# Storing gates and spatial results in turned blocks, and a new order of the attention

## The chip, the cores and the metric

The kernel runs on one core of a Trainium2 chip. The metric is the device time of one execution in microseconds. [...]

## The reference

One layer of a decoder trunk with 512 tokens of 2048 channels, in float32. A vector `c` conditions the layer. Two token mixers stand side by side, a latent attention and a chunked spatial gating unit, and a learned gate each merges them:

```python
mod = silu(c) @ w_ada + b_ada;  shift, scale, gate = split(mod, 3)
h = rmsnorm(x, attn_norm_g) * (1 + scale) + shift
q_lat, kv_lat, k_rope, z_mla, u, v, z_sgu, g_mla, g_sgu = split(h @ w_in)
q = rmsnorm(q_lat) @ w_uq           # 16 heads, 128 plain + 64 rotary columns
kv = rmsnorm(kv_lat) @ w_ukv        # 16 heads, 128 key + 128 value columns
y_mla = causal_attention(q, k, v_mla) * silu(z_mla)
y_sgu = u * (tril(w_spatial) @ rmsnorm(v) + b_spatial) * silu(z_sgu)   # chunks of 128 tokens
merged = sigmoid(g_mla) * y_mla + sigmoid(g_sgu) * y_sgu
out = rmsnorm(x + gate * (merged @ w_out), final_norm_g)
```

## The kernel before

Every float32 product is made of three products of a reduced type: each operand is split into a high part (a cast on ScalarE) and a low part (the rest, a subtraction on VectorE). A 128-column slice of weights against 512 tokens is one matmul of 512 columns.

The kernel has three long stages. The first projects the latents and some plain columns. The **block stage** makes the wide projections v, u, the three gate inputs and the two z with fewer products than the plain way: seven products of half size in place of eight, so that a block of two groups of 512 channels runs through 28 steps (the list `V7`) of twelve matmuls each. Eleven blocks (`BLOCKS`) follow one another. Around each step, a dictionary of events, filled by a planner that spreads the work with `place` and `on`, tells what ScalarE, VectorE and the queues do in that step; events of the phase `LOAD` are transfers on SP's queue. Weights are loaded some five steps before their first use. Results of a group of four heads are kept in two tiles `held[...]` of [128 tokens, 2, 512 channels], one for each half of the tokens. For c in 0 to 3, `t_store` writes the finished spatial results to `t_d[c]` in DRAM, and for c in 0 to 2, `g_out` writes the finished gate of the attention branch (silu of z times sigmoid of g) to `gt_d[c]`; each is one transfer of 512 KB for each half. The last gate, c = 2, is finished only when the attention begins, by the list `last_gates`.

The **attention** takes the 16 heads in order. Its matmuls in head h are: the scores of head h; in an odd head the values of two heads (`vproj`); the query projection of head h + 1 (`qproj`); in an even head the rotary projection of the next pair (`rproj`); the key projection of head h + 1 (`kproj`); and the product of head h - 1's shares with its values (`pv`). Each engine works through its queue in the order in which the program writes it. The softmax adds a mask, finds the maximum, takes exponentials (ScalarE, with their sums), turns the shares in blocks of 32 x 32 on VectorE and stores them to `p_d`; `turned_load` brings them back so that the blocks stand in turned places, `turned_split` makes high and low parts of them on ScalarE and GpSimd, and `pv` uses them one head later. The spatial results come back in the same way: `fetch_blocks` loads each head's [channels, tokens] tile in four transfers of 32 x 16 runs of 128 bytes, and VectorE turns each 32 x 32 block (L1779). The gate comes back with tokens on the partitions, in runs of 512 bytes. There the reciprocal sums of the softmax are multiplied into it (four scalings on ScalarE, L1818), and four transposes on TensorE (`turn`, L1721) bring it to [channels, tokens], with a copy out of PSUM (L1778). Heads 12 to 15 (`GATED = 12`) have a gate that is already turned; there VectorE scales the shares.

The weights of a projection come through `Stream`: three raw buffers, a high and a low part in two places, loaded by SP in order, split in order. `get(i, ahead)` asks for granule i and splits `ahead` more. `merge_a` multiplies the attention by the gate and adds the spatial result; the `finish` that it queues splits the sum later for the output projection. `pieces_at` sums the pieces of the conditioning's gate between the heads on VectorE (L148).

The third stage is the output projection (`out_granule`) with the residual and the last norm.

Of the kernel before, what the change touches and what calls it, by code (L numbers as in the profile page):

```python
# [20 lines left out]
P = 128  # L21
# [116 lines left out]
def trunk_layer(ctx, tc, xT, xn, c, vecs, pos, wada, w1, w2, wv, wv3, wv4, wh, wh15, wq, wqr, wk, wvv, wo, wsT, bsp, gfin, out,  # L138
# [106 lines left out]
    gt_d = [scratch(f"gt_d{i}", [NB, P, S]) for i in range(3)]  # L245
    t_d = [scratch(f"t_d{i}", [NB, P, S]) for i in range(4)]
# [684 lines left out]
    def g_out(c, half):  # L931
        DMA.dma_start(gt_d[c][2 * half:2 * half + 2].rearrange("n p w -> p n w"), held["z", c, half])

    last_gates = []
    for b in range(1, len(BLOCKS)):
# [21 lines left out]
        if ta == "z":  # L957
            for half in range(2):
                s_ = max(ready[ta, ca, half], ready[tb_, cb, half]) + 1
                if b == len(BLOCKS) - 1:  # L960
                    last_gates.append(lambda c=ca, half=half: (g_gate(c, half, DVE if half else nc.gpsimd), g_out(c, half)))
# [62 lines left out]
    def t_store(c, half):  # L1024
        DMA.dma_start(t_d[c][2 * half:2 * half + 2].rearrange("n p w -> p n w"), held["u", c, half])
# [12 lines left out]
    for g in range(H):  # L1038
# [433 lines left out]
    for n, tag in (("krh", "hh10"), ("krl", "hl10"), ("m1", "hh11"), ("m2", "hl11"), ("r", "hh12"), ("qsa", "hl12"),  # L1472
                   ("qsb", "hh13"), ("pt1", "hl13"), ("th0", "hh14"), ("tl0", "hl14"), ("th1", "hh15"), ("tl1", "hl15")):
        place[n] = (hp.p, tag)
    for n, tag in zip(("vh0", "vl0", "qh", "ql", "kh", "kl", "vh1", "vl1", "pt3", "pt2", "th2"), range(11)):
        place[n] = (latp.p, f"lat{tag}")
# [13 lines left out]
    for key, at_ in ready.items():  # L1490
        if at_ >= 0:
            squash(key)
# [6 lines left out]
    gd = Scope("gdots")  # L1499
    cq.clear()  # L1500
    piece_at = lambda i: piece_load(i, lambda: nt(gd.p, [P, S], F32, "piece", bufs=2))

    def pieces_at(h):
        k = n_early + sum(PIECES[:h])
        for i in range(k, k + PIECES[h]):
# [3 lines left out]
            if i > n_early and pieces[i][0] != pieces[i - 1][0]:  # L1509
                quarter_after(i)  # L1510

# [16 lines left out]
    def fetch(h):  # L1528

        gt[h] = nt((ga if h < 8 else g2p).p, [P, S], F32, f"g{h}")  # L1530
        if h < GATED:
            DMA.dma_start(gt[h].rearrange("p (n w) -> p n w", n=NB),
                          gt_d[h // 4][:, :, h % 4 * P:(h % 4 + 1) * P].rearrange("n p w -> p n w"))
# [4 lines left out]

    def fetch_blocks(h):

        vt[h] = nt(bp.p, [P, S], F32, f"b{h}")
        rows = t_d[h // 4].rearrange("n (a i) w -> i (n a) w", i=SQ)
        for b in range(P // SQ):
            o = h % 4 * P + b * SQ
            DMA.dma_start(vt[h][b * SQ:(b + 1) * SQ].rearrange("i (m j) -> i m j", j=SQ), rows[:, :, o:o + SQ])
# [16 lines left out]
    def qproj(h, meanwhile=None, then=None):  # L1562
        wH, wL = get(gq[h])
# [462 lines left out]
```

## Time and profile before

| what | us |
|---|---|
| median of 3 runs | 1538.77 (1537.94 to 1539.0) |
| profiled execution, time | 1538.12 |
| profiled execution, span | 1536.2 |
| TensorE busy | 1521.3 |
| VectorE busy | 1233.6 |
| ScalarE busy | 804.9 |
| GpSimd busy | 169.2 |

The span goes from the first to the last instruction; the profiled execution's time is 1.9 us longer. Times in the rows count from the start of the span. The block stage ends at 1072 us, the attention at about 1341 us. Ends of matmuls are modelled, so that one matmul's time overlaps the next; the pitch is read from start to start.

### The profile page before, as it was taken

What the parts mean: (1) busy time and instruction counts of PE and PEld (TensorE: products, weight loads), DVE (VectorE), ACT (ScalarE), POOL (GpSimd) and SP (SyncE); (2) the same over time, 40 slices, a digit from 0 to 9 for tenths busy, and PEclk for the clock granted to TensorE, in tenths of its full rate; (3) what the DMA queues carried; (4) which work ended last, traced back from release to release, by engine and by line L of the source; (5) the groups of instructions that cost most, each with busy time, mean ns of one, the idle gap of its engine ahead of it and who ended that gap; (6) DMA issues with size and microseconds to landing.
All of it is one profiled execution on the core that took longest, in us unless ns stands there. A gap on an engine that the chain in (4) does not pass through costs nothing.

```text
span 1536.2 us, 20578 instructions
## 1 busy us (share of the span) xinstructions
PE 1521.3 (99%) x7152; PEld 1272.9 (83%) x7152; DVE 1233.6 (80%) x1676; ACT 804.9 (52%) x1276; POOL 169.2 (11%) x161
## 2 busy tenths in 40 slices
PE   9999999999999999999999999999999999999997
PEld 7888878888888888888888888888888888888886
DVE  8989797768787889887888787878789889965753
ACT  4444555546555546455555565557666666532331
POOL 0000000101010000011010101010122223221120
PEclk9999999999999999999999999999999999999999
DMA  9979776858886786878686867777788888759832
GB/s 374 385 271 352 235 215 173 237 147 238 248 223 187 211 231 199 228 214 217 198 207 187 225 207 188 239 191 215 201 204 191 202 190 190 193 148 339 281 105 110
DMA packets 368922, 337.93 MB, mean 220 GB/s; under 512 B 133689, under 2 KB 313969, under 8 KB 363697
## 3 DMA queue, kind: packets, MB, share of 16 engines
q1 hardware_dynamic: 345906, 313.54, 66.0%
q0 software_dynamic: 22912, 23.07, 9.8%
q8 instruction: 56, 0.92, 0.3%
q14 instruction: 48, 0.39, 0.1%
HBM read 302.38 MB, written 34.17 MB: 219 GB/s over the span
## 4 chain that ended last, share of the span: by engine, by line
PE 92%; DVE 3%; DMA 2%; SPq 1%; ACT 1%; issue 1%; DVEq 0%; ACTq 0%
PE ps L1457 18%; PE ps L1458 18%; PE ps L1455 18%; PE ps L463 5%; PE ps L158 3%; PE ps L1769 3%; PE ps L1771 3%; PE ps L1772 3%; PE ps L159 3%; PE ps L157 3%; PE ps L1557 3%; PE ps L1558 2%; PE ps L1560 2%; PE ps L472 2%; PE ps L473 2%; PE ps L475 1%
## 5 line engine op out<-in xcount | busy, mean ns | idle before, releaser
L145 DVE TENSOR_TENSOR X<-X,X 128x1024 fp32r<-128x1024 f32 (+2 forms) x111 | 130.5, 1183 | 28.5 <-ACT X L694 27.1
L694 ACT CAST w0h<-X 128x1024 fp32r<-128x1024 f32 x70 | 73.6, 1052 | 95.4 <-PE ps L1458 51.8
L694 ACT CAST X<-X 128x1024 fp32r<-128x1024 f32 x70 | 73.6, 1052 | 93.7 <-PE ps L1458 56.4
L694 ACT CAST w1h<-X 128x1024 fp32r<-128x1024 f32 x69 | 72.5, 1051 | 76.0 <-PE ps L1458 39.6
L145 DVE TENSOR_TENSOR w0l<-X,w0h 128x1024 fp32r<-128x1024 f32 x70 | 85.6, 1222 | 28.5 <-ACT w0h L694 28.3
L145 DVE TENSOR_TENSOR w1l<-X,w1h 128x1024 fp32r<-128x1024 f32 x69 | 84.3, 1221 | 24.4 <-ACT w1h L694 24.4
L122 DVE TENSOR_TENSOR w1l<-wraw,w1h 128x1024 fp32r<-128x1024 f32 (+3 forms) x60 | 69.9, 1166 | 30.7 <-ACT w1h L121 22.8
L122 DVE TENSOR_TENSOR w0l<-wraw,w0h 128x1024 fp32r<-128x1024 f32 (+3 forms) x61 | 65.7, 1078 | 35.2 <-ACT w0h L121 16.9
L145 DVE TENSOR_TENSOR X<-wraw,X 128x1024 f32<-128x1024 f32 (+1 forms) x65 | 79.4, 1221 | 17.2 <-ACT X L694 16.9
L1458 PE MATMUL ps<-w1h,hl 128*128 128x512 f32 x236 | 91.8, 389 | 0.0
L1457 PE MATMUL ps<-w1h,hh 128*128 128x512 f32 x236 | 91.8, 389 | 0.0
L1457 PE MATMUL ps<-w0h,hh 128*128 128x512 f32 x236 | 91.8, 389 | 0.0
L1458 PE MATMUL ps<-w0h,hl 128*128 128x512 f32 x236 | 91.8, 389 | 0.0
L1457 PE MATMUL ps<-X,hh 128*128 128x512 f32 x232 | 90.5, 390 | 0.3 <-ACT X L694 0.3
L1458 PE MATMUL ps<-X,hl 128*128 128x512 f32 x232 | 90.3, 389 | 0.0
L148 DVE SCALAR_TENSOR_TENSOR wada<-wada,cact 128x2048 f32<-128x2048 f32 x39 | 88.9, 2283 | 0.6 <-DMA wada<-in_wada 0.6
L121 ACT CAST w0h<-wraw 128x1024 fp32r<-128x1024 f32 (+3 forms) x61 | 52.8, 866 | 69.8 <-PE ps L1772 20.6
L121 ACT CAST w1h<-wraw 128x1024 fp32r<-128x1024 f32 (+3 forms) x60 | 52.6, 877 | 56.2 <-PE ps L473 15.7
L145 DVE TENSOR_TENSOR wraw<-wraw,X 128x1024 f32<-128x1024 f32 x66 | 80.4, 1218 | 0.3 <-DMA X<-in_wh 0.3
L659 POOL DMA_DIRECT2D X<-in_wh x9 | 11.6, 1284 | 536.9 <-DVE w1l L145 178.8
L1702 POOL TENSOR_TENSOR hl<-turned,hh 128x384 fp32r<-128x384 f32 (+1 forms) x48 | 45.9, 984 | 222.1 <-ACT hh L1701 156.4
L145 DVE TENSOR_TENSOR d<-ps,d 128x512 fp32r<-128x512 f32 (+1 forms) x90 | 58.8, 682 | 8.2 <-ACT d L162 8.2
(468 smaller groups left out, 4387.6 us busy)
## 6 DMA issues: line engine op xcount, KB each, us to landing
X<-in_wh SPq DMA_DIRECT2D x131, 512.0 KB, 4.9
wada<-in_wada SPq DMA_DIRECT2D x39, 1024.0 KB, 7.6
wraw<-in_wo SPq DMA_DIRECT2D x32, 512.0 KB, 4.6
wraw<-in_wh SPq DMA_DIRECT2D x21, 512.0 KB, 4.5
wraw<-in_wh POOLq DMA_DIRECT2D x21, 512.0 KB, 7.9
turned<-p_d SPq DMA_DIRECT2D x64, 160.0 KB, 3.9
X<-in_wv SPq DMA_DIRECT2D x17, 512.0 KB, 4.4
X<-in_wh SPq DMA_DIRECT2D x22, 384.0 KB, 6.0
```

The source lines that it names most:

```text
L121: self.nc.scalar.copy(hi[:, :n], raw[:, :n])
L122: self.nc.vector.tensor_tensor(out=lo[:, :n], in0=raw[:, :n], in1=hi[:, :n].bitcast(F32), op=ALU.subtract)
L145: DVE.tensor_tensor(out=out, in0=in0, in1=in1, op=op)
L148: DVE.scalar_tensor_tensor(out=out, in0=in0, scalar=scalar, in1=in1, op0=op0, op1=op1, **kw)
L157: PE.matmul(ps, ah, bh, start=start, stop=False)
L158: PE.matmul(ps, ah, bl, start=False, stop=False)
L159: PE.matmul(ps, al, bh, start=False, stop=stop)
L463: PE.matmul(ps1[m], a[:, cols[m]], b, start=(j == 0 and a is wH and b is hh[j]), stop=False)
L694: ACT.copy(hi, t)
L1455: PE.matmul(to, xh[:, tk], wL[:, k], start=False, stop=sp, skip_group_check=True)
L1457: PE.matmul(to, xh[:, tk], wH[:, k], start=st, stop=False, skip_group_check=True)
L1458: PE.matmul(to, xl[:, tk], wH[:, k], start=False, stop=False, skip_group_check=True)
```

## The change

Stores: `g_out` and `t_store` no longer write a tile of half the tokens in one transfer. They write it in eight: for each of the two chunks of 128 tokens and each 32 tokens of it, a transfer of 32 tokens by 16 blocks of 32 channels, every block row (32 numbers, 128 bytes) to a place of its own. The scratch tensors get the shape [16 blocks of channels, 32 tokens, 16 blocks of tokens, 32 channels]. The four transfers of one chunk are issued in one step, those of the other chunk in the next.

Loads: a head's gate and its spatial result are then each one contiguous [128, 512] region of DRAM and are loaded by one transfer each. What comes in has the 32 x 32 blocks in their turned places, and VectorE turns within the blocks (`turn_blocks`), for the gate too. The transposes on TensorE, the copy out of PSUM and the scalings of the gate go. The reciprocal sums are multiplied into the shares of every head instead, on ScalarE.

Order in the attention: the splits of the next weights are written out one by one (`split_next`) in place of `ahead`; the scores begin with the rotary products; the mask and the maximum become one instruction of VectorE each (a fused addition and maximum with a wide mask in bfloat16); pieces, rotation, merging and value splits get new places; the last squashes and the last gate move behind the first head's maxima and powers; several scratch tiles get other homes. Core of the diff:

```diff
-    gt_d = [scratch(f"gt_d{i}", [NB, P, S]) for i in range(3)]
-    t_d = [scratch(f"t_d{i}", [NB, P, S]) for i in range(4)]
+    gt_d = [scratch(f"gt_d{i}", [16, 32, 16, 32]) for i in range(3)]
+    t_d = [scratch(f"t_d{i}", [16, 32, 16, 32]) for i in range(4)]
+    def turned_store(to, half, src, t):
+        for a in range(4):
+            m = 8 * half + 4 * t + a
+            DMA.dma_start(to[:, :, m].rearrange("q i j -> i q j"), src[32 * a:32 * a + 32, t].rearrange("i (q j) -> i q j", j=32))
-    def g_out(c, half):
-        DMA.dma_start(gt_d[c][2 * half:2 * half + 2].rearrange("n p w -> p n w"), held["z", c, half])
+    def g_out(c, half, t):
+        turned_store(gt_d[c], half, held["z", c, half], t)
-                on(s_ + 1, LOAD, g_out, ca, half)
+                for t in range(2):
+                    on(s_ + 1 + t, LOAD, g_out, ca, half, t)
-                on(stored[c, half], LOAD, t_store, c, half)
+                for t in range(2):
+                    on(stored[c, half] + t, LOAD, t_store, c, half, t)
-    for key, at_ in ready.items():
-        if at_ >= 0:
-            squash(key)
+    wide_mask = nt(gd.p, [P, S], BF16, "mask")
+    def turned_blocks(t, src, h):
+        DMA.dma_start(t, src[h % 4 * 4:h % 4 * 4 + 4].rearrange("b i m j -> (b i) (m j)"))
+    def split_next():
+        ws.split_to(ws.n_split)
+        ws.dma_to(ws.n_split - 1 + len(ws.raws))
+        for f, i in ((rotary, 3), (rotary, 2), (plain_, 3), (plain_, 2), (rotary, 1), (plain_, 1), (rotary, 0), (plain_, 0)):
+            f(i)
+                DVE.tensor_tensor_reduce(out=dst[i], in0=dst[i], in1=wide_mask[:, (NB - 1 - i) * P:], scale=1.0, scalar=-3.0e38,
+                                         op0=ALU.add, op1=ALU.max, accum_out=mx[:, i:i + 1])
+            for i in ((q,) if q else (1, 0)):
+                ACT.activation(pr_[i], pr_[i], AF.Copy, scale=mx[:, 4 + i:5 + i])
-    def turn(src):
-        ps = bank()
-        for n in range(NB):
-            tk = slice(n * P, (n + 1) * P)
-            PE.transpose(ps[:, tk], src[:, tk], ident)
-        return ps
+    def turn_blocks(h):
+        for t in (gt[h], vt[h]) if h < GATED else (vt[h],):
+            DVE.transpose(out=t, in_=t)
+        todo = piece_tasks(h)
+        peaks, powers, shares, send = softmax(h, scores(h))
+        if h and not odd:
+            split_next()
+        peaks()
+        if h == 0:
+            for key, at_ in ready.items():
+                if at_ >= 0:
+                    squash(key)
+        powers()
+        if h == 0:
+            for f in last_gates:
+                f()
+        if not odd:
+            if h:
+                turn_blocks(h - 1)
+            shares()
+            for q in (3, 2, 0):
+                send(q)
+            merge()
+            ps = qproj(h + 1)
+            split_next()
+            qfinish(h + 1, ps)
+            for f in todo[1:]:
+                f()
+            if h:
+                parts = turned_split(h - 1)
+            if turning and h:
+                first, swap, second = rrotate(rproj(pair))
+                first()
+                split_next()
+                swap((0, 1))
+            ps = kproj(h + 1)
+            for f in todo[:1]:
+                f()
+            kfinish(h + 1, ps)
+            split_next()
+            turned_load(h)
...
+        elif more:
+            r = second()
+            shares()
+            for q in (3, 2, 0):
+                send(q)
+            parts = turned_split(h - 1)
+            turn_blocks(h - 1)
+            merge()
+            vfinish = vproj(h // 2)
+            vfinish()
+            split_next()
+            vfinish()
+            for f in todo:
+                f()
+            ps = qproj(h + 1)
+            qfinish(h + 1, ps)
+            rfinish(pair, r)
+            split_next()
+            turned_load(h)
+            kfinish(h + 1, kproj(h + 1))
```

## Rows read from the trace of the kernel before

**Rows 1.** The page: busy us, share of the span, instructions

```profile
PE 1521.3 (99%) x7152; PEld 1272.9 (83%) x7152; DVE 1233.6 (80%) x1676; ACT 804.9 (52%) x1276; POOL 169.2 (11%) x161
```

**Rows 2.** Busy by stretch: PE, PEld, DVE, ACT, POOL; clock, DMA share, GB/s

```profile
700.00:800.00 100.00, 100.00 (x444) 82.72 (x443) 83.46 (x103) 53.21 (x75) 9.99 (x9) 1.00 0.77 207
...
1072.00:1112.00 40.00, 37.65 (x198) 32.10 (x198) 29.20 (x56) 27.67 (x57) 4.16 (x4) 1.00 0.74 190
```

**Rows 3.** TensorE's waits: us in total, times, longest us

```profile
PE ps L1557 <- ACT w0h L121: 0.8, 1, 0.8
PE ps L1640 <- DVE hl L145: 0.8, 1, 0.8
PE ps L1638 <- ACT d L162: 0.7, 1, 0.7
PE ps L1642 <- DVE d L145: 0.6, 1, 0.6
...
PE ps L1557 <- ACT w1h L121: 0.3, 1, 0.3
```

**Rows 4.** Timeline around one value product: start us, us, engine, line

```profile
1150.78 0.60 PE L1721 MATMUL ps<-ident,g 128*128 128x128 f32 x4
...
1151.14 0.48 PE L157 MATMUL ps<-hh,d 128*128 128x512 f32 x1
...
1151.45 0.40 PE L158 MATMUL ps<-hl,d 128*128 128x512 f32 x1
...
1152.56 0.68 DVE L145 TENSOR_TENSOR d<-ps,d 128x512 fp32r<-128x512 f32 x1
...
1153.09 0.45 PE L1638 MATMUL ps<-d,d 128*128 128x512 f32 x1
```

**Rows 5.** Busy us in an even and an odd head, columns as above

```profile
1150.78:1167.24 16.46, 16.46 (x85) 14.14 (x84) 15.11 (x29) 9.19 (x25) 4.83 (x4) 1.00 0.74 166
1167.24:1185.40 18.16, 18.16 (x115) 16.59 (x114) 15.73 (x33) 13.43 (x32) 4.54 (x7) 1.00 0.89 216
```

**Rows 6.** ScalarE's timeline at the start of the attention

```profile
1075.14 1.28 ACT L925 ACT_TABLE_LOAD   x1
1076.43 2.01 ACT L925 ACTIVATE d<-d 128x1024 f32<-128x1024 f32 x2
```

**Rows 7.** VectorE's groups in that pair of heads: busy us, mean ns

```profile
L145 DVE TENSOR_TENSOR ps<-ps,mask 128x128 f32<-128x128 f32 x8 | 2.3, 293 | 0.1
L122 DVE TENSOR_TENSOR w1l<-wraw,w1h 128x1024 fp32r<-128x1024 f32 x1 | 2.0, 2002 | 0.0
...
L1779 DVE STREAM_TRANSPOSE b<-b 128x512 f32<-128x512 f32 x2 | 1.4, 702 | 0.0
...
L145 DVE TENSOR_TENSOR sig<-ps,sig 128x512 f32<-128x512 f32 x2 | 1.3, 671 | 0.4 <-PE ps L159 0.4
```

**Rows 8.** The maxima (L1658) alone in that pair of heads

```profile
1150.78:1185.40 34.62, 3.93 (x8) 1.00 0.82 192
```

**Rows 9.** ScalarE's groups in that pair of heads

```profile
L1818 ACT ACTIVATE g<-g,mx 128x128 f32<-128x128 f32 x8 | 2.6, 395 | 0.0
...
L162 ACT CAST b<-sig 128x512 fp32r<-128x512 f32 x2 | 1.3, 636 | 0.0
...
L1778 ACT COPY sig<-ps 128x512 f32<-128x512 f32 x2 | 1.1, 567 | 0.0
```

**Rows 10.** DMA issues: count, KB each, median us to landing

```profile
X<-in_wh SPq DMA_DIRECT2D x131, 512.0 KB, 4.9
...
turned<-p_d SPq DMA_DIRECT2D x64, 160.0 KB, 3.9
...
t_d<-d SPq DMA_DIRECT2D x8, 512.0 KB, 6.9
```

**Rows 11.** Issue of the shares' loads (L1686): min, median, max ns

```profile
L1686 SPq DMA_DIRECT2D turned<-p_d x64: 318/898/3907, 1098.1 to 1361.8; - x64
```

**Rows 12.** Issue of the spatial results' loads (L1545)

```profile
L1545 SPq DMA_DIRECT2D b<-t_d x64: 302/487/2025, 1068.3 to 1313.3; - x64
```

More of the change, by code (lines that the diff above doesn't have):

```diff
@@ L1510, in pieces_at @@
                 quarter_after(i)
+        k = n_early + sum(PIECES[:h])
+        return [lambda i=i: one(i) for i in range(k, k + PIECES[h])]
     cq_slots = ["lat11", "lat12"]
@@ L1537, in trunk_layer @@
     SQ = 32
+    def turned_blocks(t, src, h):
+        DMA.dma_start(t, src[h % 4 * 4:h % 4 * 4 + 4].rearrange("b i m j -> (b i) (m j)"))
     def fetch_blocks(h):
         vt[h] = nt(bp.p, [P, S], F32, f"b{h}")
[L1542 to L1545, printed above, removed]
+        turned_blocks(vt[h], t_d[h // 4], h)
     for h in range(1, H):
@@ L1580, in rrotate, with swap, first, second @@
     def rrotate(src):
-        m2, r = at("m2", F32), at("r", F32)
-        swapped(m2, src)
-        rotate(r, src, at("m1", F32), m2)
-        return r
+        m1, m2, r = at("m1", F32), at("m2", F32), at("r", F32)
+        def swap(bs):
+            for b in bs:
+                s_, d_ = slice(32 * b, 32 * b + 32), slice(32 * (b ^ 1), 32 * (b ^ 1) + 32)
+                ACT.copy(m2[d_], src[s_])
+        def first():
+            tt(m1, src, tables[0], ALU.mult)
+        def second():
+            tt(m2, m2, tables[1], ALU.mult)
+            tt(r, m1, m2, ALU.add)
+            return r
+        return first, swap, second
     def rfinish(p, r):
@@ L1593, in rfinish, with kproj @@
         qs[2 * p], qs[2 * p + 1] = a, b
-    def kproj(h, ahead=1):
-        wH, wL = get(gk[h], ahead)
+    def kproj(h):
+        wH, wL = get(gk[h], 0)
         ps = bank()
@@ L1606, in vproj @@
     def vproj(p):
-        wH, wL = get(gvv[p])
+        wH, wL = get(gvv[p], 0)
         pss = []
@@ L1675, in softmax @@
-        send(3)
-        send(2)
-        normalise(0)
-        send(0)
-        return mx[:, 4:8]
+        return peaks, powers, shares, send
     def turned_load(h):
@@ L1782, in trunk_layer @@
     for h in range(H):
         more, odd, pair = h + 1 < H, h % 2 == 1, h // 2 + 1
+        turning = not odd and 2 * pair < H
         if h == H - 2:
             ring[:], n_bank[0] = [4, 5, 6, 7], 0
-        dst = scores(h)
-        turning = not odd and 2 * pair < H
-        first = (gr[pair] if h else gk[1]) if turning else gk[h + 1] if not odd else gq[h + 1] if more else go[0, 1]
-        shares_ = softmax(h, dst, lambda: ws.split_to(first))
-        if odd:
-            parts = turned_split(h - 1)
-            vproj(h // 2)
@@ L1793, in trunk_layer @@
-        if more:
-            qproj(h + 1, merge)
-            if turning and h:
-                rps = rproj(pair)
-            elif odd:
-                rfinish(pair, r)
-            if turning and h:
-                parts = turned_split(h - 1)
+        todo = piece_tasks(h)
[7 more added lines that the diff above has]
+                    squash(key)
@@ L1801, in trunk_layer @@
             turned_load(h)
             kfinish(h + 1, kproj(h + 1))
-            if not odd and not turning:
-                parts = turned_split(h - 1)
-            if h == 0:
-                rps = rproj(1)
-            if h == H - 2:
-                pso = [bank_at(k) for k in range(NB)]
-                out_granule(0, 0, pso)
-        else:
+        else:
+            shares()
+            for q in (3, 2, 0):
+                send(q)
+            parts = turned_split(h - 1)
+            vfinish = vproj(h // 2)
+            vfinish()
+            vfinish()
+            turn_blocks(h - 1)
```

154 lines of the change are left out of this document (73 added, 81 removed).

## Prediction

> **What bounds the kernel now.** I read the page first, then the busy time by stretch, then what TensorE waited for, and at the end single heads of the attention instruction by instruction. The page gives TensorE 1521.3 us of busy time in a span of 1536.2 [rows 1]. Busy is not yet bound, since a waiting matmul chain can look busy too, so the second view counts: in 100 us of the block stage TensorE issued 444 matmuls, 0.225 us each, with no idle time and the clock at 1.00, while VectorE was busy 83.46 us and the DMA engines 0.77 of the time [rows 2]. The matmuls come at one fixed pitch; nothing but fewer matmuls, or a wait that opens where there is none, changes that stage. The first 40 us of the attention are the exception, with 37.65 us busy.
>
> The third view says where TensorE stood still in or near the attention: five waits, 0.8 + 0.7 + 0.8 at its start, 0.6 + 0.3 in its last heads, 3.2 us in all [rows 3]. Around each wait the pipeline drains and refills, which I put at 0.25 us: a lone matmul starts 0.31 us before its successor after a break in the stream, against 0.225 in the run [rows 2, 4]. So some 4.5 us of the attention is standstill. Between those places it runs without a gap, head after head, 16.46 us for an even and 18.16 us for an odd one [rows 5]. VectorE is the engine next to it: 15.11 and 15.73 us busy in the same heads, so 1.35 and 2.43 us free. ScalarE has far more room.
>
> **What the change takes from TensorE.** In each of heads 0 to 11 four transposes turn the gate. They start at 1150.78 and the first matmul behind them at 1151.14: 0.36 us; that matmul then holds the engine 0.31 us instead of 0.225, as the first behind another kind of instruction [rows 4]. Per head 0.36 + 0.08 = 0.44 us, and 12 x 0.44 = 5.3 us. The stretch lies on the path that sets the end (no gap before or behind it), so this is time, not cover. No projection, score or value matmul is added or removed; the scores are only reordered (rotary terms first). Reordering alternates widths of 512 and 384 columns; nothing shows a price for that, so I take 0, with 16 x 0.05 = 0.8 us as the most (the 0.08 step seen above, in half the heads' switches).
>
> **The start of the attention.** The three waits there are for ScalarE and VectorE, and the table load of 1.28 us and the two wide squashes of 2.01 us lie in ScalarE's queue just before [rows 6]. The change moves both behind the first head's maxima, and issues the rotary products first, two blocks of which (2 x 0.225 + 2 x 0.175 = 0.8 us, the narrower by its columns) need only the rotated queries. Head 0 now loses 0.8 + 0.7 + 0.5 for two restarts = 2.0 us. After: the last key projection ends, its copy takes 0.6 and the low part 0.7, 1.3 us plus hand-over, against 0.8 of rotary cover and 0.45 of the first two plain products; 0.3 to 0.5 us of wait stay. What goes is not all gained: squashes and table load (3.3 us), and a second table load for the exponentials, now stand in ScalarE's queue ahead of head 0's powers, and behind the powers and four scalings waits the split of the rotary weights that the third projection needs. Adding up that queue from the key's copy: two weight splits 1.5, squashes 3.3, load 1.28, powers 2.0, scalings 1.7, split 0.85, together 10.6 us from about the time at which the scores can go on; scores and two projections ahead of that use cover 2.8 + 4.1 + 2.7 = 9.6. I take 1.2 us of new wait there, where the old order lost 0.8 + 0.25 one head later. Start: 3.1 before, 1.6 after, gain 1.5 us; bounds 0 and 3.1.
>
> **The last heads.** The waits of 0.6 and 0.3 are for VectorE and for a weight split that comes late on ScalarE [rows 3]. In the new order that split is issued before the head's maxima, and VectorE no longer scales the shares of heads 12 to 15. I take 1.0 of the 1.4 us (waits and restarts); bounds 0 and 1.4.
>
> **VectorE and ScalarE in the steady heads.** Removed from VectorE per head: four mask additions of 0.293 and four reductions, 3.93 / 2 = 1.96, together 3.14 us [rows 7, 8]. Added: four fused passes. The trace has no such instruction. Below, it can't be cheaper than an addition of two sources from PSUM, 0.671 us at 512 columns; above, the pair it replaces. The nearest row is the addition, so 0.67 + 0.55 + 0.42 + 0.29 = 1.93 and 0.1 each for the read of the result, 2.3 us. Added besides: the gate's transpose, 0.70. Balance -0.84 + 0.70 = -0.14 us per head up to head 11, at worst +0.70. ScalarE loses the copy of the turned gate (0.567) and four scalings of it (4 x 0.395, overlapped 1.28), and gains four scalings of the shares (0.636 for 512 columns from SBUF, 0.395 for 128, 1.7 to 2.0 in all) [rows 9]: nothing. Heads get 0.44 us shorter, so VectorE has 1.05 and 2.1 us left.
>
> Free time does not say that nothing waits, so I laid the queues of one pair side by side with these durations. Even head, from its first score: maxima end at 5, powers at 6, three transposed blocks leave by 9, the share splits start at 10, the key's low part is done near 16.7, its use by the next head's third kind of product near 17.2. Before, that low part was done at 1152.56 + 0.68 = 1153.24 and the scores started at 1153.09, the product that reads it being the fifth, 4 x 0.225 + 0.08 = 0.98 later [rows 4]: 0.8 us of margin then, 0.5 to 1 now. Odd head: exponentials start some 3 us earlier than now, since pieces and rotation stand behind them; the key's weights are split by 11.2 against a use at 13.0. Tightest is the even head's value product: GpSimd's low parts end at 14.1 to 15.3, used at 15.4. Nothing opens by this count, but three margins lie under 1.5 us, and VectorE's low parts have taken 2.0 us where 1.2 is usual [rows 7]. I take 0.
>
> **The stores of the block stage.** Seven stores of a channel group (four results, three gates) each go from 2 transfers of 512 KB, runs of 2 KB, to 16 of 64 KB in runs of 128 bytes: 8192 runs, 512 for each of 16 DMA engines. In the attention a load of 4 x 64 KB in such runs becomes one of 256 KB in runs of 2 KB, and the gate's likewise: relief where nothing waits for it, price 0. The queue of SP gets 98 more issues; the existing loads of the same shape (512 runs) need 0.487 us each [rows 12], so eight take 4 us, spread by the change over two steps of 12 x 0.225 = 2.7 us. That fits. The engines' price: no row shows a write of 128 bytes. Reads: the shares' load has 1280 runs, 80 per engine, and is issued in 0.898 us (11 ns a run, when the queue behind moves on), landed in 3.9 (49 ns) [rows 10, 11]. The bounds are 11 and 49; I take 15, as issue back to back is the nearer case to eight stores in a row. Then a group costs 7.7 us of all engines. It has 4 steps, 10.9 us, in which 0.23 is idle (2.5 us), and 4 us of the old wide store fall away (1 MB at the stretch's 207 GB/s over 0.77): 6.5 us. Backlog 1.2 us. Weights are issued five steps before their first use and land in 4.9 us [rows 10], 13.6 - 4.9 = 8.7 us of cover. So 0 here; the price that breaks it is (6.5 + 8.7) / 512 = 30 ns a run. The third gate's stores fall into head 0, in front of loads that are wanted some 10 us later: 0.
>
> [...]
>
> **Sum.** The profiled execution took 1538.12 us (span 1536.2), the median of the runs is 1538.77, 0.65 more. 1538.1 - 5.3 - 1.5 - 1.0 = 1530.3; with 0.65 back, **1531.0 us**, 0.5% faster. A measurement here tells 0.2%, 3.1 us, from no change.
>
> **Rivals.** *The short writes choke the block stage* (the case that ends slower). Mechanism: runs of 128 bytes written cost more than 30 ns, the weight loads behind them come late, and TensorE waits at the six groups inside the stage. At the upper bound of 49 ns a group is 25 us, less 6.5 and 8.7 of cover: 9.9 us of wait each, 59 in all, 1538.8 - 7.8 + 59 = 1590. At 35 ns it is 2.7 each, 16 us: 1547. For it: the stage already uses 0.77 of the DMA time, and a 512 KB store lands in 6.9 us where the share loads need 3.9 [rows 10]. Against: 11 ns issue. Chance 0.13.
> *VectorE becomes the bound in the attention.* If the fused pass costs as much as what it replaces, and margins of 0.5 us close, each even or odd pair waits about 0.6 to 0.8 us; 7 pairs, 4 to 5.5 us, which eats the transposes: 1535 to 1537. For it: 92% busy, long queue chains. Against: the same engine was as busy before without one wait. Chance 0.14.
> *The transposes were hidden anyway*, the matmuls behind them waiting for GpSimd's low parts: only the waits go, 1536.3. Against: those parts end before, and no wait is shown. Chance 0.03.
> My forecast, 1528 to 1534.5, has 0.70.
>
> **The numbers.** Floor: all 4.5 us of waits go, 1538.8 - 5.3 - 4.5 = 1529, less some for the profile's own spread: 1528. Upwards, 0.70 + 0.17 is reached by 1537; taking in the first part of the store rival, 1540. Faster by over 0.2% means under 1535.7: 0.70 and a third of the second rival, 0.75. Same: the rest of that rival, the third, 0.11; slower: 0.13 and a touch, 0.14.
>
> **What would show it.** Right: no transposes on TensorE in the attention; an even head at 16.0 and an odd one at 17.7 us; the first 40 us of it with about 1.5 us less idle; block stage without a TensorE gap at the store steps. Wrong: waits for VectorE's low parts in every second head; TensorE waiting for weights within 20 us of a store; a fused pass of over 1 us at 512 columns; the wait of head 0 larger than 1.2 us. The forecast hangs most on the price of a short write and on margins under 1 us.

## The result and the profile after

The changed kernel is slower: 1542.76 us median of 11 runs (1540.14 to 1546.45) against 1538.60 (1537.71 to 1539.45) for the kernel before; ratio 1.0027, 95% interval 1.0018 to 1.0037. So it lost 0.27%, clear of the spread. The forecast was 1531.0 with a range of 1528 to 1540. The profiled execution took 1543.73 us, with a span of 1540.9. Each kernel has one profile, and the changed kernel's times lie 6.3 us apart, so a single wait of a few tenths in one trace need not stand in every run.

The page's first part, which answers to [rows 1], shows nothing that would explain a loss: 48 transposes fewer, VectorE 11 us less busy, ScalarE 12 us more.

```profile
PE 1520.7 (99%) x7104; PEld 1270.1 (82%) x7104; DVE 1222.5 (79%) x1656; ACT 816.6 (53%) x1280; POOL 173.5 (11%) x163
```

So I set the starts of the same matmuls in both traces side by side. Each column is the time from the start of the row above it (the first row counts from the start of the span); a head is taken at the first matmul of its scores. The last column is the last kernel but one of the experiments below.

| to | before | after | difference | e10_best |
|---|---|---|---|---|
| attention's first matmul | 1072.27 | 1075.92 | +3.65 | 1072.12 |
| head 1 | 27.03 | 27.03 | 0.00 | 25.37 |
| head 3 | 35.60 | 40.20 | +4.60 | 34.82 |
| head 13 (five pairs) | 173.18 | 170.21 | -2.97 | 168.48 |
| head 15 | 36.77 | 35.56 | -1.21 | 35.06 |
| last matmul | 183.24 | 183.26 | +0.02 | 183.26 |
| end of the span | 8.1 | 8.7 | +0.6 | 8.3 |

Two places lose: the block stage and heads 1 and 2. The steady heads gain as forecast. Here are an odd and an even head of the changed kernel, by busy time in the stretch (columns as in [rows 2], the answer to [rows 5]): 17.68 and 16.01 us, where 17.7 and 16.0 had been forecast, and no idle time in either.

```profile
1143.15:1160.83 17.68, 17.68 (x113) 16.15 (x112) 15.80 (x32) 12.44 (x29) 4.48 (x5) 1.00 0.71 170
1160.83:1176.84 16.01, 16.01 (x82) 13.78 (x82) 14.83 (x30) 10.86 (x26) 5.42 (x5) 1.00 0.91 231
```

TensorE's waits of the changed kernel (us in total, times, longest) stand against [rows 3]. The five of [rows 3] are gone. New are the first three and most of the one for `X`, a weight tile of the block stage (0.3 of its 0.9 us lies at that stage's start in both kernels); the second and `X` lie in the block stage.

```profile
PE ps L1568 <- ACT w1h L121: 4.0, 2, 3.7
PE ps L158 <- DVE vl L145: 1.8, 2, 0.9
PE ps L1568 <- ACT w0h L121: 1.3, 1, 1.3
...
PE ps L1465 <- ACT X L699: 0.9, 2, 0.6
```

**The block stage.** Before, 500 to 600 us had no idle time:

```profile
500.00:600.00 100.00, 100.00 (x442) 82.55 (x441) 87.98 (x102) 54.20 (x75) 5.16 (x4) 1.00 0.74 210
```

Now the same stretch has 2.39 us idle, and the timeline of TensorE puts the gaps at 560.79 (0.88 us, `vl`), 581.33 (0.58, `X`) and 585.52 (0.93, `vl`); `vl` is the low part of the spatial unit's operand.

```profile
500.00:600.00 100.00, 97.61 (x428) 79.44 (x427) 83.78 (x98) 52.37 (x74) 5.16 (x4) 1.00 0.78 205
```

SP's queue in the timeline some 20 us ahead of the first gap (start, us that the issues hold the queue): four times four short stores, with the load of that operand (`lat<-v_d`) between them. The 16 issues hold the queue for 16.0 of 21.3 us.

```profile
533.53 3.83 SPq L251 DMA_DIRECT2D t_d<-d  x4
537.97 5.05 SPq L251 DMA_DIRECT2D t_d<-d  x4
543.12 1.48 SPq L989 DMA_DIRECT2D lat<-v_d  x1
544.64 3.83 SPq L251 DMA_DIRECT2D t_d<-d  x4
...
551.48 3.32 SPq L251 DMA_DIRECT2D t_d<-d  x4
```

Over the kernel, the issue of one of these stores takes, at the median, more than the 487 ns of a load of the same shape [rows 12] (min/median/max ns, by line and tensor):

```profile
L251 SPq DMA_DIRECT2D t_d<-d x64: 332/657/2214, 533.5 to 868.9; - x64
L251 SPq DMA_DIRECT2D gt_d<-d x48: 319/520/2472, 924.9 to 1102.4; - x48
```

**Heads 1 and 2.** The timeline of SP's queue in head 0 has the last gate's 16 stores in one piece, 9.07 us, ahead of the stores of head 0's shares, which VectorE had turned by 1098.5, and of four loads that bring the shares back:

```profile
1093.86 9.07 SPq L251 DMA_DIRECT2D gt_d<-d  x16
1103.33 0.38 SPq L1702 DMA_DIRECT2D p_d<-hh  x1
1103.82 1.01 SPq L1702 DMA_DIRECT2D p_d<-hl  x2
...
1107.43 5.86 SPq L1711 DMA_DIRECT2D turned<-p_d  x4
```

ScalarE's timeline goes on from there. In an odd head the program has it split the shares first (L1726) and the weights of the next key projection after (L121); it stands 6.44 us. The releaser that the row names is a weight load issued just behind the shares'; the split reads `turned`, whose last issue ends at 1113.3.

```profile
1117.18 1.63 ACT L1726 CAST d<-turned 128x128 fp32r<-128x128 f32 x5 [6.44 <-DMA wraw<-in_wqr]
1118.72 0.57 ACT L162 CAST d<-ps 128x512 fp32r<-128x512 f32 x1
1119.19 0.62 ACT L121 CAST w1h<-wraw 128x512 fp32r<-128x512 f32 x1
```

In head 3, where nothing is disturbed, the first of these waits 0.34 us for its load, and the weights follow in time:

```profile
1151.33 1.64 ACT L1726 CAST d<-turned 128x128 fp32r<-128x128 f32 x5 [0.34 <-DMA turned<-p_d]
...
1153.87 0.62 ACT L121 CAST w1h<-wraw 128x512 fp32r<-128x512 f32 x1
```

And TensorE, in its timeline, waits 3.71 us for the weight split of head 1:

```profile
1119.86 0.80 PE L1568 MATMUL ps<-hh,w1h 128*128 128x512 f32 x1 [3.71 <-ACT w1h L121]
```

The wait is not all of the price. Busy time of TensorE by stretch of 2 us, with the granted clock behind it, shows the clock at 0.50 for 4 us after the stop:

```profile
1116.00:1118.00 2.00, 0.15 (x1) 1.00 1.03 341
1118.00:1120.00 2.00, 0.14 (x1) 0.65 0.81 272
1120.00:1122.00 2.00, 2.00 (x5) 0.50 0.00 0
1122.00:1124.00 2.00, 2.00 (x6) 0.50 0.57 170
1124.00:1126.00 2.00, 2.00 (x8) 0.65 0.26 92
1126.00:1128.00 2.00, 2.00 (x14) 1.00 0.82 190
```

From head 1 to head 3 the kernel takes 40.20 us where an undisturbed pair takes 33.69: 6.5 us for a wait of 3.7. All of it lies in head 1, which takes 24.19 us and, in e2_wide_last_gate below, 17.62; the rest is matmuls at the lower clock, every 0.43 us where the pitch is 0.23 at 1.00, and the restart: the first matmul behind the stop starts 0.60 us before the next.

### The profile page after: what moved, and what is told of

Read it like the earlier page. It is cut to its first block, busy times and chain, and to the rows that moved or that the text cites. A ratio compares the mean times of both kernels' runs of the same rounds, so it can differ in the third digit from the quotient of the medians.

```text
span 1540.9 us, 20572 instructions
## 1 busy us (share of the span) xinstructions
PE 1520.7 (99%) x7104; PEld 1270.1 (82%) x7104; DVE 1222.5 (79%) x1656; ACT 816.6 (53%) x1280; POOL 173.5 (11%) x163
## 5 line engine op out<-in xcount | busy, mean ns | idle before, releaser
L121 ACT CAST w0h<-wraw 128x1024 fp32r<-128x1024 f32 (+3 forms) x61 | 52.7, 864 | 71.3 <-PE ps L1787 20.7
L122 DVE TENSOR_TENSOR w0l<-wraw,w0h 128x1024 fp32r<-128x1024 f32 (+3 forms) x61 | 61.7, 1012 | 34.0 <-ACT w0h L121 16.6
L121 ACT CAST w1h<-wraw 128x1024 fp32r<-128x1024 f32 (+3 forms) x60 | 52.5, 875 | 54.5 <-PE ps L478 15.7
L122 DVE TENSOR_TENSOR w1l<-wraw,w1h 128x1024 fp32r<-128x1024 f32 (+3 forms) x60 | 63.5, 1058 | 20.1 <-ACT w1h L121 12.9
L1727 POOL TENSOR_TENSOR d<-turned,d 128x384 fp32r<-128x384 f32 (+1 forms) x48 | 43.1, 926 | 209.4 <-ACT d L1726 195.2
L1463 PE MATMUL ps<-w0l,hh 128*128 128x512 f32 x236 | 63.2, 389 | 0.0
```

The lines of the kernel that those rows point to most:

```text
L121: self.nc.scalar.copy(hi[:, :n], raw[:, :n])
L122: self.nc.vector.tensor_tensor(out=lo[:, :n], in0=raw[:, :n], in1=hi[:, :n].bitcast(F32), op=ALU.subtract)
L1463: PE.matmul(to, xh[:, tk], wL[:, k], start=False, stop=sp, skip_group_check=True)
L1727: nc.gpsimd.tensor_tensor(out=lo, in0=src, in1=hi.bitcast(F32), op=ALU.subtract)
```

## Experiments

Three theories stood against each other at first. S: the short stores cost, by their place in SP's queue, in the block stage and in head 0. N: the new order by itself, with the split of the shares ahead of the split of the weights on ScalarE, makes the wait in head 1, whatever the stores do. L: the whole loads are what lets the new order work. Later Q took N's place: ScalarE's queue passes a late load of the shares, whatever made it late, on to the weights, because the split of the shares stands ahead of theirs. All changes below are made to the changed kernel unless another is named; the diffs are cut to their core, `...` standing for what is left out.

### All stores wide again: e1_wide_all

```diff
+WIDE = (0, 1, 2)
...
+        elif t == 0:
+            DMA.dma_start(gt_d[c][2 * half:2 * half + 2].rearrange("n p w -> p n w"), held["z", c, half])
...
-        turned_store(t_d[c], half, held["u", c, half], t)
+        DMA.dma_start(t_d[c][2 * half:2 * half + 2].rearrange("n p w -> p n w"), held["u", c, half])
...
+    def wide_blocks(t, src, h):
+        rows = src.rearrange("n (a i) w -> i (n a) w", i=SQ)
+        for b in range(P // SQ):
+            o = h % 4 * P + b * SQ
+            DMA.dma_start(t[b * SQ:(b + 1) * SQ].rearrange("i (m j) -> i m j", j=SQ), rows[:, :, o:o + SQ])
```

With `wide_blocks` each head's gate and spatial result come in four transfers in place of one.

> All stores as before (two transfers of 512 KB a group), each head's gate and spatial result loaded in four transfers of 128-byte runs, attention as in the changed kernel. Theory S (the short-run stores hold SP's queue: about 3.2 us of waits in the block stage and 6.5 us in head 1): both go, median near 1533, no wait over 0.5 us on TensorE between 500 and 600 us, head 1 without the wait of 3.7 us and without the half clock. Rival N (the new order itself, share splits ahead of weight splits on ScalarE, makes the wait in head 1): the wait of 3.7 us stays, median near 1539.5. Rival L (the relief of whole loads is what carries the new order): single heads get longer by 0.3 us or more, median over 1536.

Measured: 1544.7 us (1541.22 to 1545.96), ratio 1.0037 (1.0025 to 1.0050). S had expected 1533: a miss, and by the time alone L's figure, over 1536, came out. The block stage is clean again (500 to 600 us: 100.00 of 100 busy) and head 1 has no wait (17.62 us), so S holds in both places and N, which had the wait of head 1 stay, does not. But TensorE now waits for weights in heads 0, 3, 5 and 7, 6.7 us in all:

```profile
PE ps L1577 <- ACT w1h L122: 4.6, 3, 2.5
PE ps L1577 <- ACT w0h L122: 2.1, 1, 2.1
```

ScalarE's timeline in head 3 shows the same order of events as in head 1 of the changed kernel, with no short store anywhere:

```profile
1144.53 1.63 ACT L1735 CAST d<-turned 128x128 fp32r<-128x128 f32 x5 [3.53 <-DMA turned<-p_d]
...
1147.06 0.62 ACT L122 CAST w1h<-wraw 128x512 fp32r<-128x512 f32 x1
```

### Only the last gate wide: e2_wide_last_gate

The same with `WIDE = (2,)` and `t_store` left short: heads 8 to 11 load their gate in four transfers.

> Only the last gate (stored at the start of the attention) goes back to two wide stores and four loads a head for heads 8 to 11. Theory S: the shares of head 0 are no longer stored behind 9.1 us of short-run stores, head 1 loses its 6.5 us, the waits of the block stage stay: median near 1536. Rival N: no change from the changed kernel, near 1542.5.

Measured: 1537.07 us (1535.54 to 1538.82), ratio 0.9988 (0.9979 to 0.9997). The wait of 3.7 us is gone, those of the block stage stay (1.51, 0.46 and 0.93). As S expected, but for 1 us; N had expected no change.

### All wide but the last gate: e3_wide_but_last

The same with `WIDE = (0, 1)` and `t_store` wide.

> The counterpart: spatial results and the first two gates go back to wide stores, the last gate keeps its sixteen short-run stores. Theory S: block stage without waits, the 6.5 us of head 1 stay: median near 1539.5. If the block stage's waits come from something else than these stores they stay, and the median is near 1542.5.

Measured: 1548.99 us (1548.36 to 1550.15), ratio 1.0068 (1.0056 to 1.0081), where S had 1539.5: a miss. The block stage is clean, but the waits for `w1h` come to 6.8 us in five heads, and one of 2.3 us for `w0h` stands in head 0. With e1 this seemed to say that the order needs the whole loads (L); the last experiment corrects that.

### Stores spread over twice the steps: e4_spread

The last gate is wide as in e2; of the other short stores (those of `t_d[3]` excepted) two are issued in a step in place of four.

```diff
...
+                store_at = s_ + 1 if half == 0 else max(s_ + 1, store_at + 4)
+                for i in range(4):
+                    on(store_at + i, LOAD, g_out, ca, half, i // 2, range(i % 2 * 2, i % 2 * 2 + 2))
...
+                for i in range(4):
+                    on(stored[c, half] + i, LOAD, t_store, c, half, i // 2, range(i % 2 * 2, i % 2 * 2 + 2))
```

> Last gate wide as in the run before; the other short-run stores are issued two in a step over eight steps in place of four in a step over two to four (the last group of spatial results excepted). Theory S with SP's queue as the place: two issues of about 1 us fit a step of 2.7 us, the waits of the block stage go, median near 1533. If the DMA engines' backlog and not the issue is what is late, the same runs cost the same engine time: waits of 1 to 3 us stay, median 1534 to 1536.

Measured: 1538.5 us (1536.68 to 1542.02), ratio 1.0003 (0.9994 to 1.0012). Both forecasts, 1533 and 1534 to 1536, are missed. The gap at 561 us is gone, a wait of 0.94 for `vl` stays, and two new ones of 0.50 and 0.44 us open near 940 and 1023 us, where a copy of ScalarE (L915) starts late. That the tile it writes was still being stored would fit SP's stores there; the row names no store, so this is not shown. No gain by the median.

### Half of the last gate by GpSimd's queue: e5_last_gate_pool

```diff
+            by(a).dma_start(to[:, :, m].rearrange("q i j -> i q j"), src[32 * a:32 * a + 32, t].rearrange("i (q j) -> i q j", j=32))
...
+    BY = lambda c, half: lambda a: nc.gpsimd if c == 2 and half == 0 else DMA
...
-        turned_store(gt_d[c], half, held["z", c, half], t)
+        turned_store(gt_d[c], half, held["z", c, half], t, BY(c, half))
```

> The changed kernel, but the eight short-run stores of the last gate's first half go out on GpSimd's queue; the other eight stay on SP's. Same bytes, same runs, same loads. If SP's queue is the place (head 0's shares stand behind the stores): the shares leave some 4.5 us earlier, the wait of 3.7 us in head 1 falls under 0.5 and the half clock goes, median near 1537. If the DMA engines' backlog is the place: the shares' way back stays late, a wait of 2 us or more stays, median over 1540.

Measured: 1540.41 us (1538.54 to 1542.11), ratio 1.0011 (1.0002 to 1.0020). Same bytes, same short runs, another queue for half of the last gate: SP is held 5.16 us where it was 9.07, head 0's shares leave 3.1 us earlier (1100.21), and the wait of 3.71 falls to 0.56. ScalarE starts to split the shares at 1113.93 in place of 1117.18. So it is the place in the queue, not the runs' time on the engines, that hurts head 1. The median is another matter: 2.4 us below the changed kernel's, where the queue theory had 1537 and its rival over 1540. Short waits stand in heads 2, 4, 7, 8 and 14, between 0.25 and 0.62 us each.

### Half of all short stores by GpSimd's queue: e6_half_pool

```diff
+    BY = lambda c, half: lambda a: nc.gpsimd if (half == 0 if c == 2 else a > 1) else DMA
...
-        turned_store(t_d[c], half, held["u", c, half], t)
+        turned_store(t_d[c], half, held["u", c, half], t, lambda a: nc.gpsimd if a > 1 else DMA)
```

> As the run before, and in the block stage two of each four short-run stores go out on GpSimd's queue. Queue theory: SP is held 2 us a step in place of 4, the waits for the spatial unit's operand at 560 and 585 us go, median 1533.5 to 1535. Engine theory: the waits stay, 1537 or more. A third way: GpSimd's own accumulating loads come late behind the stores, new waits of the block stage for weights, over 1538.

Measured: 1536.4 us (1535.13 to 1537.87), ratio 0.9986 (0.9977 to 0.9995). 500 to 600 us is busy for 99.80 us: the waits go as the queue theory has it, while the median lies between its 1533.5 to 1535 and its rival's 1537. SP's timeline has the load of the spatial unit's operand leave at 539.21, where it was 543.12:

```profile
539.21 0.47 SPq L991 DMA_DIRECT2D lat<-v_d  x1
```

The first group's eight stores on SP now take 10.0 us in place of 16.0 for sixteen, so 1.25 us each where it was 1.00: fewer stores free the queue, but each holds it longer. What stays lies in the attention, and ScalarE's timeline shows one of these waits as before: the shares' load is late by itself, and the weights stand behind it.

```profile
1212.82 1.63 ACT L1728 CAST d<-turned 128x128 fp32r<-128x128 f32 x5 [3.67 <-DMA turned<-p_d]
1214.36 0.61 ACT L162 CAST b<-sig 128x512 fp32r<-128x512 f32 x1
...
1215.36 0.62 ACT L121 CAST w1h<-wraw 128x512 fp32r<-128x512 f32 x1
```

TensorE's row for that projection carries the delay:

```profile
1216.03 0.50 PE L1570 MATMUL ps<-hh,w1h 128*128 128x512 f32 x1 [1.49 <-ACT w1h L121]
```

The second queue brought no faster transfer: the median time to landing of these stores rose from 5.0 (`t_d`) and 4.3 us (`gt_d`) in the changed kernel to between 5.6 and 7.5. For one store of `gt_d` the issue is small beside the transfer (0.52 us against 4.3 to landing in the changed kernel, both medians); but for 16 in a row it is 9.07 us in which nothing else leaves SP's queue, and that was the price in head 1.

### The kernel before with the gate's part alone: e7_gates_old_order

The kernel before, its order of the attention kept; the gates are stored short, loaded whole and turned by VectorE, the shares are scaled on ScalarE, the transposes go.

```diff
...
-            gate_ = nt(tp, [P, S], F32, "sig", bufs=3)
-            ACT.copy(gate_, turn(gt[h]))
+            DVE.transpose(out=gt[h], in_=gt[h])
...
-                g_ = gt[h][:, n * P:(n + 1) * P]
-                ACT.activation(g_, g_, AF.Copy, scale=shares_[:, n:n + 1])
...
+                ACT.activation(pr_[q], pr_[q], AF.Copy, scale=mx[:, 4 + q:5 + q])
```

> The kernel before with the gates' part alone: gates stored in short runs, loaded whole and turned by VectorE, shares scaled on ScalarE, no transposes on TensorE; spatial results, fused maximum and order of the attention as before. If the transposes are time and the old order has room: heads 0.44 us shorter, the five old waits stay, median 1533 to 1535. If the longer way from powers to stored shares (four scalings, 1.8 us) or the last gate's stores don't fit the old order: waits in every second head or in head 1, median 1537 to 1541.

Measured: 1584.61 us (1583.88 to 1587.9), ratio 1.0303 (1.0289 to 1.0317), far above both forecasts. Nearly every head now waits for weights:

```profile
PE ps L1562 <- ACT w1h L121: 18.1, 14, 2.0
PE ps L1562 <- ACT w0h L121: 10.2, 8, 1.6
PE ps L1647 <- DVE d L145: 4.5, 6, 0.7
```

ScalarE's timeline in heads 10 and 11 shows why. The old order scales two blocks of the shares right behind their powers, and the weights' split stands behind that scaling; the next two scalings wait for a reciprocal that stands in VectorE's queue behind the low part of those weights and the turning of the first shares.

```profile
1293.56 1.23 ACT L1658 ACTIVATE d<-d,mx 128x512 f32<-128x512 f32 x2 [0.25 <-DVE mx L1656]
1294.69 0.82 ACT L121 CAST w1h<-wraw 128x768 fp32r<-128x768 f32 x1
...
1297.66 0.80 ACT L1658 ACTIVATE hl<-hl,mx 128x256 f32<-128x256 f32 x2 [1.35 <-DVE mx L1656]
```

In TensorE's timeline that is a wait for the same weights:

```profile
1295.56 0.50 PE L1562 MATMUL ps<-hh,w1h 128*128 128x512 f32 x1 [1.98 <-ACT w1h L121]
```

ScalarE does not wait for the shares' load in this pair of heads. So it is again the place in ScalarE's queue: the scalings need an order that splits the weights ahead of them. What the transposes alone are worth this run does not show.

### The shares split behind the weights: e8 and e9

One move in the odd heads, in e8_half_pool_shares_later on top of e6_half_pool, in e9_shares_later on the changed kernel:

```diff
-            parts = turned_split(h - 1)
             turn_blocks(h - 1)
             merge()
             vfinish = vproj(h // 2)
             vfinish()
             split_next()
+            parts = turned_split(h - 1)
             vfinish()
```

> e6_half_pool with one move: in the odd heads the shares of the next pair are split behind the next weights' split instead of ahead of it. Theory Q (in ScalarE's queue the split of the key's weights stands behind the shares' load, so a late load becomes a wait of TensorE for weights): the wait of 1.49 us for w1h near 1216 us goes, the sum of TensorE's waits in the attention falls from about 3.7 us to 2.2 us, the profile is 1.3 to 1.6 us shorter (about 1533.7 us) and the median about 1534.5 to 1535.5 us. Rival D (the loads are late however the queue stands): the wait moves to the value products, which then wait for GpSimd's low parts of the shares, and the median is 1536.4 us or above.

> The changed kernel with the same move only; its last gate's stores still stand in SyncE's queue ahead of head 0's shares. Theory Q: the wait of 3.71 us in head 1 for the key's weights goes, at most 2 us of it come back at the value product of head 2, TensorE's clock does not fall to 0.50 for six microseconds, and the median is about 1538 us (3.5 to 5 us below the changed kernel); the block stage's waits of about 2.4 us stay. Rival D: the wait only moves and keeps its size, the clock falls as before, and the median stays within 1 us of 1542.8 us.

Measured: e8 1531.41 us (1529.58 to 1533.42), ratio 0.9956 (0.9942 to 0.9969); e9 1536.29 us (1534.52 to 1539.96), ratio 0.9986 (0.9977 to 0.9995). Q is borne out by both, and by more than it expected: by the medians e8 lies 5.0 us below e6, e9 6.5 below the changed kernel. In e9 the 16 stores still hold SP's queue for 8.86 us and ScalarE still waits 3.46 us for the shares, but the key's weights are now split 4.1 us ahead of the shares, where they were split 2.0 us behind them:

```profile
1111.50 0.62 ACT L121 CAST w1h<-wraw 128x512 fp32r<-128x512 f32 x1 [0.88 <-PE ps L159]
1115.58 1.63 ACT L1726 CAST d<-turned 128x128 fp32r<-128x128 f32 x5 [3.46 <-DMA turned<-p_d]
```

The waits that come back, 0.57 and 0.76 us, are not at the value product, where I had put them, but at head 2's scores, for VectorE's low parts; one of 0.30 us for GpSimd's low parts of the shares follows at the value product. Why e8 gained more than the wait of 1.49 us that it removed: a wait costs more than its row says. In e6 the two pairs with waits took 36.35 and 36.45 us, where e8 has 33.69 and 35.05, 4.1 us in all, and the rows of these waits name 1.49 + 0.29 + 0.64 = 2.4 us.

### Head 0's rotary weights ahead of its shares: e10_best

```diff
+            if h == 0:
+                ps = qproj(1)
+                split_next()
             shares()
             for q in (3, 2, 0):
                 send(q)
             merge()
-            ps = qproj(h + 1)
-            split_next()
+            if h:
+                ps = qproj(h + 1)
+                split_next()
```

> e8_half_pool_shares_later with the query projection of head 1 and the split of its rotary weights put ahead of the four scalings of head 0's shares. Theory Q: the wait of 1.30 us for w0h in head 0 falls below 0.3 us, and the median is 1.0 to 1.3 us below e8's, about 1533.5 to 1534.5 us. Rival D: the shares of head 0 are scaled and stored some 2 us later, their load is late by as much, and the wait comes back in head 1 or at the first value product: the median is that of e8 or above.

Measured: 1529.79 us (1528.87 to 1530.78), ratio 0.9943 (0.9930 to 0.9955), 1.6 us below e8 by the median, though the two sets of five runs overlap. The wait of 1.30 us is gone and head 0 is 1.64 us shorter than in e8; two waits of 0.30 us come in head 2, which is 1.19 us longer. So by the profiles this move is worth some 0.5 us. This kernel is faster than the one before and the changed one. Its first 40 us of the attention have no idle time, against [rows 2]:

```profile
1072.00:1112.00 40.00, 40.00 (x211) 34.29 (x210) 30.77 (x59) 31.79 (x64) 10.05 (x13) 1.00 0.77 205
```

### No short store, and the better order: e11_wide_all_shares_later

e1_wide_all with the two moves of e10_best.

> e1_wide_all (no short stores at all, every head's gate and spatial result loaded in four transfers) with the two moves of the order that e10_best has: the shares split behind the next weights' split in the odd heads, and head 0's rotary weights split ahead of its shares. Theory Q (what cost was ScalarE's queue, and the short stores cost only their own time on the queues): the waits for w0h and w1h that e1 had (2.08, 1.31, 0.77 and 2.48 us) go, the median falls from e1's 1544.7 us to about 1532 to 1535 us, and the turned storing has little or no part in what e10_best gains. Rival L (the whole loads carry the new order: with four loads in place of one the shares come too late wherever they are split): the value products wait for the shares' low parts or the merges for their operands, and the median stays above 1537 us, 7 us or more over e10_best.

Measured: 1534.35 us (1533.7 to 1535.84), ratio 0.9971 (0.9959 to 0.9983). Q, not L: e1's 6.7 us of waits for weights are gone, and the median falls by 10.3 us, though ScalarE still waits 0.88, 2.26, 2.83 and 1.64 us for the shares' load in heads 3, 5, 7 and 9. What is left on TensorE are short waits, 0.64, 0.75 and 0.22 us for `hl`, a low part from VectorE, at the scores of two even heads and three of 0.30 us for `rx`, GpSimd's low parts of the shares. From head 1 to head 15 it takes 242.38 us and e10_best 238.36. So what turned storing is worth, once its issues are shared between two queues, is some 4.0 us in the heads, by the profiles, and 4.6 by the medians. The rest of the change with the two moves (no transposes, scaled shares, fused maxima, the order), without the turned stores, already beats the kernel before by 0.3%.

## Why the prediction was wrong, point by point

- **Transposes, -5.3.** Right. e10_best takes 168.48 us for the five pairs from head 3 to head 13, before 173.18: 4.70 for ten heads, 0.47 each, where 0.44 was forecast. That it is the transposes and not the order shows in the kernel before: its head 13 turns no gate and takes 17.71 us, where its odd heads that do take 18.18; the new order's odd head takes 17.68. The changed kernel kept 2.97 of it, having two waits of 0.3 us there that with their restarts cost some 1.5.
- **Steady heads, 0.** The step that failed. The walk along the queues had "the key's weights are split by 11.2 against a use at 13.0". The time is right for a steady head: in head 3 the split ends 11.3 us behind the first score. But the walk names no load, and the split of the shares, which stands in ScalarE's queue ahead of that weight split in the odd heads, waits for one. In head 3 it already waits 0.34 us for it, so the load had no margin, and the 1.8 us of the walk hold only for a load that comes in time. In head 1 of the changed kernel, behind the 16 stores, ScalarE waited 6.44 us, and TensorE 3.71. e9 and e11 show it: loads that are late again, with the two splits exchanged, do not stop TensorE for weights.
- **The third gate's stores in head 0, "in front of loads that are wanted some 10 us later: 0".** The other half of the same failure. What stood behind the 16 issues was not only loads but the stores of head 0's own shares, and behind these their loads. The 16 issues held the queue 9.07 us, where the prediction's 0.487 us each gives 7.8; the size was near, and what it delays was not looked up. e2 and e5 show it: with these stores wide, or half of them on another queue, the wait of 3.71 is gone or 0.56. Either change, to the stores or to the order of the splits, removes it; the two together made +4.60 between heads 1 and 3, where -0.88 (two heads' transposes) and -1.05 (the old wait in head 1) had been counted.
- **Stores of the block stage, 0.** Mis-sized, and the victim was another one. The sum let "eight take 4 us", 0.487 each, and called that a fit. The first group's issues took 0.83 to 1.26 us each (means of four), 3.3 to 5.1 us for the four of one step of 2.7, and the load of the spatial unit's operand, queued between them, came late. Only this group opened gaps, mostly for that operand and not for weights. The loss is 3.65 us up to the attention, of which 0.23 was there before the first block (219.36 against 219.59 us); the rest is the shown 2.39 with their restarts. The 15 ns for a run on the engines no run measures by itself. The time of the queue alone, spread over 32 runs for each of 16 engines, would be 26 to 39 ns a run in that group and 20 at the median, by my estimate, about the 30 at which the sum said it would break. The rival had 16 us at 35 ns, since it let all six groups wait. That the held queue is the place is what e6 shows: the same stores on two queues leave 0.20 us of idle time in that stretch. Whether full engines are what draws the issues out stays open, since in e6 each took longer on SP.
- **Whole loads, "relief where nothing waits for it, price 0".** Too low once the order is right: 4.0 us between e11 and e10_best from head 1 to head 15.
- **Start of the attention, -1.5.** Half right. The new wait in head 0 was forecast at 1.2 us and measured 1.30. It cost 1.66 us up to head 1, judged by e10_best, which has no wait there, and took back the whole gain at head 0's scores (0.88 us): 0.00 there in place of -0.4. The other part of the term, the old wait of 0.83 us in head 1 with its restart, did go: head 1 took 19.15 us before and 17.62 in e2, some 1.0 more than its transposes account for. In the changed kernel the wait of 3.71 us covers it.
- **Last heads, -1.0.** Right: -1.21 from head 13 to head 15.
- **VectorE.** Right. By groups of VectorE, in the pair of heads above, the fused pass took 0.69 us at 512 columns, where 0.67 was taken, and the read of its result 0.14 where 0.1 was; VectorE was busy 30.63 us in the pair, before 30.84 [rows 5], and it did not become the bound. It is next in line: once the weights came in time, waits for its low parts came up (0.57 and 0.76 us in e9).

```profile
L1683 DVE CUSTOM_DVE_ANT_0 ps<-ps,mask 128x512 f32<-128x512 f32 x2 | 1.4, 691 | 0.0
...
L1683 DVE DVE_READ_ACCUMULATOR2_ANT mx<- 128x1 f32 x8 | 1.1, 141 | 0.0
```

With the queues put right the sum comes near: e10_best's profiled execution took 1529.3 us, the forecast for a profiled execution was 1530.3. In part that is luck, for e10_best is another kernel and its parts miss both ways: -1.66 up to head 1 where -0.4 was counted, -0.78 in heads 1 and 2 where -1.9 was, -1.71 in the last heads where -1.0 was.

Left open: why the four loads of the shares, in the changed kernel, hold SP's queue 5.86 us in head 0 when the median is 0.73 each. The short stores ahead of them are not the whole reason, since the same four hold it 4.74 us in e2, which has none there, and those of head 6 hold it 6.22 us in e6, far from any short store, just ahead of the wait of 1.49 us. Not tried: the last gate's stores behind head 0's shares on SP's queue.

## What to carry to other kernels

When a transfer is cut into many short runs, count the time for which its issues hold the queue, and list what stands behind them there, stores of the next step included. When walking an in-order queue, mark each instruction that waits for a DMA and ask what stands behind it that needs none; put that first: the exchange was worth 5.0 and 6.5 us here, against 1.6 us of other waits that came up in e9 and none in e8. The same holds for work that is added to the queue, as e7's scalings ahead of the weights show. Price a wait of a saturated TensorE at more than its row: 1.30 us cost 1.66, and 3.71 cost 6.5, as the clock fell to 0.50.

## What the runs showed of the hardware

- After the stop of 3.71 us in head 1 the granted clock stood at 0.50 from 1120 to 1124 us, and at 0.65 in the stretches on either side; matmuls of 512 columns came every 0.43 us there and every 0.23 before. After e6's stop of 1.49 us the granted clock stayed at 1.00; after one of 2.48 us in e1_wide_all matmuls of 512 columns came every 0.43 us from 1221.33 to 1223.46 us and every 0.23 from 1223.85.
- One store of 64 KB in runs of 128 bytes held SP's queue 0.33 to 2.2 us, median 0.66 (`t_d`); in e6_half_pool, with half of them on each queue, the issues took 0.33 to 2.3 us, median 0.95, on SP and 0.65 to 1.60, median 0.88, on GpSimd.
- The times of the changed kernel spread over 6.3 us in 11 runs, those of e10_best over 1.9 in 5, and those of the kernel before over 1.7 in 11.
